# Half-height products alternated between the two row halves of TensorE, and attention scores as three float32r products

## The chip, the cores and the metric

The kernel runs on one core of a Trainium2 chip. The metric is the device time of one execution in microseconds (us); lower is better. Engines are named as in the profile: PE is TensorE's matmul stream, PEld its weight loads, DVE VectorE, ACT ScalarE, POOL GpSimd, SP the queue of SyncE that issues DMAs.

## The reference

One decoder block on 512 tokens of width 1024. A combined input projection feeds two mixers side by side, differential attention ("da", 4 heads of two 64-wide halves) and RWKV-7 time mixing ("rw", 8 heads of 64); then an output projection, a PEER retrieval over 16384 experts, an embedding gate and a last norm. What the change touches is in the mixers:

```python
# diff_attention, one block of 128 queries (h = 4 heads, c = 2 halves of 64)
s = jnp.einsum('bhcqd,bhckd->bhcqk', qb, k).astype(f32)
pr = jax.nn.softmax(jnp.where(causal, s, -jnp.inf), axis=-1)
a = pr[:, :, 0] - lam * pr[:, :, 1]
return jnp.einsum('bhqk,bhkv->bhqv', a.astype(v.dtype), v)

# rwkv7_mix, one token
sa = jnp.einsum('bhij,bhj->bhi', state, -kk_t)
state = (state * d_t[:, :, None, :] + sa[..., None] * (kk_t * a_t)[:, :, None, :]
         + v_t[..., None] * k_t[:, :, None, :])
return state, jnp.einsum('bhij,bhj->bhi', state, r_t)
```

## The kernel before

Tokens are handled in four blocks b = 0 to 3 of 128. The kernel is written in a tile framework: at build time a scheduler fixes the order of instructions on each engine, and pools hand out memory pages; a tile that is given a page used before waits for the last reader of the old tile. At run time every engine works through its own list in order. Two tags of pages carry the mixers: `p2` (128 x 512 floats, 28 pages) and `p4` (128 x 1024 floats, 14 pages).

The mixers take the first 436 us or so of the program. Up to about 142 us the rw columns are projected. Then, for each b, `rw_prepare(b)` computes decays and keys (matmuls plw, pla, pcum, prem; DVE ops e_ex, ka, zs, aa, be, kt), transposes four tiles to 64-row layout (ptr: be, e_ex, e_in, kt), multiplies them per head (psA, 64 rows each: the heads of even number use the upper row half of TensorE, s = 0, those of odd number the lower, s = 1), masks the results on DVE (aab, arb, aak, ark) and multiplies with the values (pg, copied out as akv). Matmuls acc of the da projections are woven between as filler for PE; `da_prepare(b)` applies rope and transposes queries and keys (ptq, copied into qT and kT). Psum tiles of psA, pg, py and most others share the tag "mm", which has two banks.

The triangular systems of the rw mixer are solved on DVE: `rw_solve(half)` loads both blocks' masked products (sol_u) and runs 31 steps of one multiply (sol_p) and one reduce (sol_x), one after the other, with results sent out over DRAM (td, read back as tt). `rw_solve(0)` serves b = 0, 1; the table `PACE = (0, 0, 4, 0)` offers its steps while `rw_prepare(2)` is written. `rw_solve(1)` serves b = 2, 3 and is offered with the first attention heads. Its sol_u lies in a p4 page, its sol_p in a p2 page.

From about 277 us on, per b: attention scores psS (four heads times c = 0, 1; 64-row matmul of up to 512 keys, then a 128-row matmul that adds the causal mask, then max on DVE and exp on ACT into a p4 tile pexp), pta and po for the values; and for rw: pwu, pmt, prp, then per 32-token chunk the state update pst and at the end the output py (L702 at full height, L710 on 64 rows and 32 columns). Matmuls accr of another projection are filler here.

Of the kernel before, what the change touches and what calls it, by code (L numbers as in the profile page):

```python
# [8 lines left out]
F32 = mybir.dt.float32  # L9
F32R = mybir.dt.float32r  # L10
# [8 lines left out]
T = 512  # L19
# [35 lines left out]
class Kernel:  # L55
# [347 lines left out]
    def p2(self, name, shape=(128, 512), dt=F32):  # L403
        return self.pages.tile(list(shape), dt, name=name, tag="p2", bufs=28)

    def p4(self, name, shape=(128, 1024), dt=F32):
        return self.pages.tile(list(shape), dt, name=name, tag="p4", bufs=14)
# [48 lines left out]
    def rw_prepare(self, b, psum, r, k, v, kk, lx, st):  # L456
# [85 lines left out]
        for lhs, d0, d1 in ((bet, aab, st["arb"]), (ktt, aak, ark)):  # L542
            for m2 in range(2):
                for s in range(2):
                    q = slice(64 * s, 64 * s + 64)
                    ps = psum.tile([128, 2, 2, 128], F32, name="psA", tag="mm")
                    for mm in range(2):
                        m = 2 * m2 + mm
                        nc.tensor.matmul(ps[:, mm, :, :], lhs[q, m * 128:(m + 1) * 128], art[q, m, :, :],  # L549
                                         start=True, stop=True)  # L550
                    h = slice(4 * m2 + s, 4 * m2 + s + 3, 2)
                    nc.vector.tensor_tensor(d0[:, h, :], ps[:, :, 0, :],
                                            self.mask2[:, None, 0, :].to_broadcast([128, 2, 128]), op=OP.mult)
                    nc.vector.tensor_tensor(d1[:, h, :], ps[:, :, 1, :],
                                            self.mask2[:, None, 1, :].to_broadcast([128, 2, 128]), op=OP.mult)
# [127 lines left out]
    def rw_out(self, b, st, psum, out):  # L683
# [14 lines left out]
        for par in range(2):  # L698
            py = psum.tile([128, 4, 64], F32, name="py", tag="mm")
            o = slice(64 * par, 64 * par + 64)  # L700
            for m in range(4):
                nc.tensor.matmul(py[:, m, :], st["arb"][:, 2 * m + par, :], st["wu"][:, 1, 2 * m + par, :],  # L702
                                 start=(m == 0), stop=False, skip_group_check=True)
            for c in range(4):
# [3 lines left out]
                q = slice(32 * c, 32 * c + 32)  # L708
                for m in range(4):
                    nc.tensor.matmul(py[q, m, :], st["rp"][o, m, q], s[o, m, :], start=False,  # L710
                                     stop=(m == 3), skip_group_check=True)
            nc.vector.tensor_tensor(y[:, par:8:2, :], py, yk[:, par:8:2, :], op=OP.add)
# [15 lines left out]
    def da_prepare(self, b, z, zT, psum):  # L728
# [16 lines left out]
        if isinstance(zT, list):  # L745
            for i, x in enumerate(zT):
                nc.scalar.activation(x[:, :, b * 128:b * 128 + 128], pt[:, 2 * i:2 * i + 2, :], AF.Copy)
        else:
            nc.scalar.activation(zT, pt, AF.Copy, scale=0.125)

    def da_block(self, b, qT, kT, vs, psum, out):
# [7 lines left out]
        for h in range(4):  # L759
            pq = self.p4("pexp", [128, 2, 512])  # L760
            p = [pq[:, 0], pq[:, 1]]
            for c in range(2):
                o = slice(64 * c, 64 * c + 64)
                ps = psum.tile([128, 512], F32, name="psS", tag="acc", bufs=4)
                nc.tensor.matmul(ps[:, :nk], qT[o, h, :], kT[h // 2][o, h % 2, :nk], start=True, stop=True)  # L765
                nc.tensor.matmul(ps[:, b * 128:nk], self.ident_r, self.causal, start=False, stop=True,
                                 skip_group_check=True)
                mx = st[:, c, h:h + 1]
                nc.vector.tensor_reduce(mx, ps[:, :nk], axis=AX.X, op=OP.max, negate=True)
                nc.scalar.activation(p[c][:, :nk], ps[:, :nk], AF.Exp, bias=mx, accum_out=st[:, 2 + c, h:h + 1])  # L770
# [839 lines left out]
```

## Time and profile before

| | |
|---|---|
| median of three executions | 1839.75 us (1837.05 to 1845.11) |
| profiled execution | 1837.09 us, span 1835.4 us |
| granted clock of PE, mean over the span | 0.969 |
| PE busy | 1728.9 us (94%) |
| DVE busy | 1425.6 us (78%) |
| ACT busy | 746.7 us (41%) |
| POOL busy | 604.7 us (33%) |

Busy shares are means over the whole program; the mixers are its first quarter, and only there do the two builds differ in the order of their instructions. A busy PE is not PE at its peak: records of pipelined matmuls overlap, so what a matmul costs is read from the distance between starts.

### The profile page before, as it was taken

How to read it: one execution, taken by the hardware profiler on the slowest of the kernel's cores; microseconds unless marked ns; L12 is line 12 of the kernel's file. 1: busy time of each engine (PE TensorE's matmuls, PEld its weight loads, DVE VectorE, ACT ScalarE, POOL GpSimd, SP SyncE). 2: the span in 40 equal slices, each digit the busy share in tenths (PEclk: the TensorE clock that was granted, in tenths of full speed). 3: DMA queues.
4: the chain of work that ended last, by engine and by line, in shares of the span. 5: the costliest groups of instructions: out<-in, count | busy, mean ns of one | idle time of the engine just before them, and what ended most of it. 6: DMA issues, size and time to landing. Idle time of an engine off the chain costs nothing.

```text
span 1835.4 us, 28662 instructions
## 1 busy us (share of the span) xinstructions
PE 1728.9 (94%) x10458; PEld 1468.2 (80%) x10458; DVE 1425.6 (78%) x3216; ACT 746.7 (41%) x1382; POOL 604.7 (33%) x425
## 2 busy tenths in 40 slices
PE   7889996998899888999999999999999999999998
PEld 6766764766777787998777888889899999999986
DVE  5366787675569998888888888887888888888885
ACT  5353332432345654444344333333333333333354
POOL 2650011111046663001111133234545555555530
PEclk9896996999999999999999999999999999999999
DMA  7451233433332343446666587778989898989891
GB/s 232 137 149 55 75 114 79 129 80 127 117 120 71 125 127 115 132 139 216 206 209 197 187 272 249 254 246 292 313 302 317 300 316 303 312 303 316 303 332 58
DMA packets 150417, 363.71 MB, mean 198 GB/s; under 512 B 43922, under 2 KB 58510, under 8 KB 150148
## 3 DMA queue, kind: packets, MB, share of 16 engines
q1 hardware_dynamic: 113412, 227.65, 38.7%
q0 software_dynamic: 36864, 134.23, 21.5%
q8 instruction: 82, 1.34, 0.3%
q14 instruction: 59, 0.48, 0.1%
HBM read 332.61 MB, written 21.36 MB: 193 GB/s over the span
## 4 chain that ended last, share of the span: by engine, by line
PE 67%; DVE 19%; issue 3%; ACT 3%; POOL 0%; DMA 0%; SPq 0%; DVEq 0%; ACTq 0%; POOLq 0%
PE po L1278 21%; PE phid L1142 8%; PE phid L1144 8%; PE phid L1143 8%; PE pg L1247 2%; DVE wlo L133 2%; PE psA L549 2%; DVE ids L1091 2%; ACT whi L129 1%; DVE rest L985 1%; PE psS L765 1%; DVE jj L1235 1%; PE accr L239 1%; PE accr L237 1%; PE accr L238 1%
## 5 line engine op out<-in xcount | busy, mean ns | idle before, releaser
L133 DVE TENSOR_TENSOR wlo<-wraw,whi 128x1024 fp32r<-128x1024 f32 x243 | 297.5, 1224 | 150.6 <-ACT whi L129 150.5
L129 ACT ACTIVATE whi<-wraw 128x1024 fp32r<-128x1024 f32 x276 | 291.4, 1057 | 171.3 <-PE phid L1143 59.0
L1144 PE MATMUL phid<-u2dhi,wlo 128*128 128x384 f32 x1024 | 347.3, 339 | 12.8 <-POOL wlo L133 12.8
L1142 PE MATMUL phid<-u2dhi,whi 128*128 128x384 f32 x1024 | 350.4, 342 | 1.0 <-ACT row L1151 1.0
L1143 PE MATMUL phid<-u2dlo,whi 128*128 128x384 f32 x1024 | 346.4, 338 | 0.0
L1301 POOL DMA_INDIRECT row<-in_peer_u_dram,idx x128 | 189.8, 1483 | 403.2 <-DVE row L1313 219.7
L1301 POOL DMA_INDIRECT row<-in_peer_v_dram,idx x128 | 186.1, 1454 | 277.0 <-DVE h L1317 194.7
L1278 PE MATMUL po<-whi,chi 128*128 128x512 f32 x768 | 243.9, 398 | 1.2 <-ACT row L1151 1.2
L1278 PE MATMUL po<-whi,clo 128*128 128x512 f32 x768 | 243.1, 398 | 1.7 <-DVE clo L135 0.4
L1278 PE MATMUL po<-wlo,chi 128*128 128x512 f32 x768 | 241.4, 395 | 0.0
L1144 PEld LDWEIGHTS phid<-u2dhi,wlo 128*128 128x128 f32 x1024 | 194.3, 190 | 14.8 <-POOL wlo L133 14.7
L1142 PEld LDWEIGHTS phid<-u2dhi,whi 128*128 128x128 f32 x1024 | 194.6, 190 | 5.8 <-ACT row L1151 1.3
L1143 PEld LDWEIGHTS phid<-u2dlo,whi 128*128 128x128 f32 x1024 | 194.1, 190 | 3.7
L1278 PEld LDWEIGHTS po<-whi,clo 128*128 128x128 f32 x768 | 143.0, 188 | 42.3 <-DVE clo L135 9.0
L1278 PEld LDWEIGHTS po<-wlo,chi 128*128 128x128 f32 x768 | 144.4, 188 | 34.2
L1317 DVE SCALAR_TENSOR_TENSOR h<-row,ids,h 128x1024 f32<-128x1024 f32 x128 | 164.0, 1281 | 1.6
L129 ACT ACTIVATE chi<-gelu 128x384 fp32r<-128x384 f32 x128 | 67.4, 526 | 240.1 <-DVE gelu L1255 121.8
L1278 PEld LDWEIGHTS po<-whi,chi 128*128 128x128 f32 x768 | 141.1, 188 | 25.6 <-ACT row L1151 1.5
L1313 DVE SCALAR_TENSOR_TENSOR row<-row,xn 128x1024 f32<-128x1024 f32 x128 | 153.7, 1220 | 0.0
L1151 ACT ACTIVATE gelu<-phid 128x384 f32<-128x384 f32 x86 | 42.3, 492 | 266.9 <-PE phid L1144 266.9
L133 POOL TENSOR_TENSOR wlo<-wraw,whi 128x1024 fp32r<-128x1024 f32 x33 | 78.4, 2386 | 126.4 <-ACT whi L129 114.7
L201 PE MATMUL acc<-whi,uhi 128*128 128x512 f32 (+1 forms) x224 | 89.6, 404 | 16.7 <-ACT whi L129 9.5
(439 smaller groups left out, 2884.7 us busy)
## 6 DMA issues: line engine op xcount, KB each, us to landing
wraw<-in_peer_uT_dram SPq DMA_DIRECT2D x128, 512.0 KB
wraw<-in_peer_v_dram SPq DMA_DIRECT2D x128, 512.0 KB
wraw<-in_w_in_dram SPq DMA_DIRECT2D x24, 512.0 KB
wraw<-in_peer_w_q_dram SPq DMA_DIRECT2D x16, 512.0 KB
ahead<-row SPq DMA_DIRECT2D x42, 192.0 KB
gelu<-ahead SPq DMA_DIRECT2D x42, 192.0 KB
wraw<-in_w_out_dram SPq DMA_DIRECT2D x8, 512.0 KB
zp<-z SPq DMA_DIRECT2D x12, 224.0 KB
```

What stands on the lines that cost most here:

```text
L129: self.last_hi = nc.scalar.activation(hi, src, AF.Copy, **({} if g is None else {"scale": g}))
L133: self.last_lo = eng.tensor_tensor(lo, src, hi.bitcast(F32), op=OP.subtract)
L201: nc.tensor.matmul(o, hi[:, k, s], whi, start=(k == 0), stop=False)
L549: nc.tensor.matmul(ps[:, mm, :, :], lhs[q, m * 128:(m + 1) * 128], art[q, m, :, :], start=True, stop=True)
L1142: nc.tensor.matmul(ps, whi[:, s], hi[:, k, :], start=(k == 0), stop=False)
L1143: nc.tensor.matmul(ps, whi[:, s], lo[:, k, :], start=False, stop=False)
L1144: nc.tensor.matmul(ps, wlo[:, s], hi[:, k, :], start=False, stop=(k == KC - 1))
L1151: nc.scalar.activation(g, ps, AF.Gelu)
L1278: nc.tensor.matmul(outs[b, e], lhs[:, s], rhs[:, 512 * e:512 * e + 512], start=(c == 0 and rhs is vhi and lhs is chi), stop=(c == NKEY - 1 ...
L1301: nc.gpsimd.indirect_dma_start(out=row, out_offset=None, in_=a["peer_u" if kind == "U" else "peer_v"], in_offset=bass.IndirectOffsetOnAxis ...
L1313: nc.vector.scalar_tensor_tensor(row, row, 1.0, xn0, op0=OP.mult, op1=OP.mult, accum_out=hid0[:, k:k + 1])
L1317: nc.vector.scalar_tensor_tensor(acc0, row, hid0[:, k:k + 1], acc0, op0=OP.mult, op1=OP.add)
```

## The change

Four edits. psA: both psum tiles of a pair are taken first, and the matmuls are written in turn for the upper and the lower row half. py: the same for the two parities of heads, with the 32-column chunks rotated. Scores: queries and keys are split into a float32r high part and a float32r rest (helper `split`, an ACT copy and a DVE subtraction), and each score is hi x hi + hi x lo + lo x hi, written in turn for c = 0 and 1 with a psum bank for each; the two causal additions follow both. Pages: qT takes 8 p2 pages in place of 4 and kT 4 p4 pages in place of 2; the pools are changed to 26 p2 and 15 p4, which are the same bytes. What is left for other tiles falls from 24 to 18 p2 pages and from 12 to 11 p4 pages.

```diff
@@ -401,10 +401,10 @@
         nc.scalar.activation(self.cos.rearrange("p b j -> p (b j)"), x0, AF.Sin)
 
     def p2(self, name, shape=(128, 512), dt=F32):
-        return self.pages.tile(list(shape), dt, name=name, tag="p2", bufs=28)
+        return self.pages.tile(list(shape), dt, name=name, tag="p2", bufs=26)
 
     def p4(self, name, shape=(128, 1024), dt=F32):
-        return self.pages.tile(list(shape), dt, name=name, tag="p4", bufs=14)
+        return self.pages.tile(list(shape), dt, name=name, tag="p4", bufs=15)
 
     def shift_group(self, rs, alloc, g0, n):
 
@@ -541,18 +541,21 @@
         st["arb"] = p4("arb", [128, 8, 128])
         for lhs, d0, d1 in ((bet, aab, st["arb"]), (ktt, aak, ark)):
             for m2 in range(2):
+
+                ps = [psum.tile([128, 2, 2, 128], F32, name="psA", tag="mm") for s in range(2)]
+                for mm in range(2):
+                    m = 2 * m2 + mm
+                    for s in range(2):
+                        q = slice(64 * s, 64 * s + 64)
+                        nc.tensor.matmul(ps[s][:, mm, :, :], lhs[q, m * 128:(m + 1) * 128], art[q, m, :, :],
+                                         start=True, stop=True)
                 for s in range(2):
-                    q = slice(64 * s, 64 * s + 64)
-                    ps = psum.tile([128, 2, 2, 128], F32, name="psA", tag="mm")
-                    for mm in range(2):
-                        m = 2 * m2 + mm
-                        nc.tensor.matmul(ps[:, mm, :, :], lhs[q, m * 128:(m + 1) * 128], art[q, m, :, :],
-                                         start=True, stop=True)
                     h = slice(4 * m2 + s, 4 * m2 + s + 3, 2)
-                    nc.vector.tensor_tensor(d0[:, h, :], ps[:, :, 0, :],
+                    nc.vector.tensor_tensor(d0[:, h, :], ps[s][:, :, 0, :],
                                             self.mask2[:, None, 0, :].to_broadcast([128, 2, 128]), op=OP.mult)
-                    nc.vector.tensor_tensor(d1[:, h, :], ps[:, :, 1, :],
-                                            self.mask2[:, None, 1, :].to_broadcast([128, 2, 128]), op=OP.mult)
+                    nc.vector.tensor_tensor(
+                        d1[:, h, :], ps[s][:, :, 1, :], self.mask2[:, None, 1, :].to_broadcast([128, 2, 128]),
+                        op=OP.mult)
             yield
             if lhs is bet:
 
@@ -695,21 +698,24 @@
         nc.gpsimd.tensor_tensor(bvf, bvf, self.ln_b, op=OP.add)
         y = self.p2("y", [128, 8, 64])
         yk = st["yk"].rearrange("p (h v) -> p h v", h=8)
-        for par in range(2):
-            py = psum.tile([128, 4, 64], F32, name="py", tag="mm")
-            o = slice(64 * par, 64 * par + 64)
-            for m in range(4):
-                nc.tensor.matmul(py[:, m, :], st["arb"][:, 2 * m + par, :], st["wu"][:, 1, 2 * m + par, :],
+        py = [psum.tile([128, 4, 64], F32, name="py", tag="mm") for par in range(2)]
+        for m in range(4):
+            for par in range(2):
+                nc.tensor.matmul(py[par][:, m, :], st["arb"][:, 2 * m + par, :], st["wu"][:, 1, 2 * m + par, :],
                                  start=(m == 0), stop=False, skip_group_check=True)
-            for c in range(4):
+
+        for m in range(4):
+            for i in range(8):
+                par = i % 2
+                c = (i // 2 + 2 * par) % 4
                 s = st["s"][c]
                 if s is None:
                     continue
-                q = slice(32 * c, 32 * c + 32)
-                for m in range(4):
-                    nc.tensor.matmul(py[q, m, :], st["rp"][o, m, q], s[o, m, :], start=False,
-                                     stop=(m == 3), skip_group_check=True)
-            nc.vector.tensor_tensor(y[:, par:8:2, :], py, yk[:, par:8:2, :], op=OP.add)
+                o, q = slice(64 * par, 64 * par + 64), slice(32 * c, 32 * c + 32)
+                nc.tensor.matmul(py[par][q, m, :], st["rp"][o, m, q], s[o, m, :], start=False,
+                                 stop=(m == 3), skip_group_check=True)
+        for par in range(2):
+            nc.vector.tensor_tensor(y[:, par:8:2, :], py[par], yk[:, par:8:2, :], op=OP.add)
         mean = sm.tile([128, 8], F32, name="mean")
         nc.vector.tensor_reduce(mean, y, axis=AX.X, op=OP.add)
         nc.vector.tensor_scalar(mean, mean, 1.0 / 64, None, op0=OP.mult)
@@ -742,11 +748,13 @@
         pt = psum.tile([128, 4, 128], F32, name="ptq", tag="tp")
         for h in range(4):
             nc.tensor.transpose(pt[:, h, :], z[:, h * 128:(h + 1) * 128], self.ident)
-        if isinstance(zT, list):
-            for i, x in enumerate(zT):
-                nc.scalar.activation(x[:, :, b * 128:b * 128 + 128], pt[:, 2 * i:2 * i + 2, :], AF.Copy)
+        hi, lo = zT
+        if isinstance(hi, list):
+            for i in range(2):
+                d = slice(b * 128, b * 128 + 128)
+                self.split(hi[i][:, :, d], lo[i][:, :, d], pt[:, 2 * i:2 * i + 2, :])
         else:
-            nc.scalar.activation(zT, pt, AF.Copy, scale=0.125)
+            self.split(hi, lo, pt, g=0.125)
 
     def da_block(self, b, qT, kT, vs, psum, out):
 
@@ -759,15 +767,21 @@
         for h in range(4):
             pq = self.p4("pexp", [128, 2, 512])
             p = [pq[:, 0], pq[:, 1]]
+
+            ps = [psum.tile([128, 512], F32, name="psS", tag="acc", bufs=4) for c in range(2)]
+            for i, j in ((0, 0), (0, 1), (1, 0)):
+                for c in range(2):
+                    o = slice(64 * c, 64 * c + 64)
+                    nc.tensor.matmul(ps[c][:, :nk], qT[i][o, h, :], kT[j][h // 2][o, h % 2, :nk],
+                                     start=i + j == 0, stop=i == 1)
             for c in range(2):
-                o = slice(64 * c, 64 * c + 64)
-                ps = psum.tile([128, 512], F32, name="psS", tag="acc", bufs=4)
-                nc.tensor.matmul(ps[:, :nk], qT[o, h, :], kT[h // 2][o, h % 2, :nk], start=True, stop=True)
-                nc.tensor.matmul(ps[:, b * 128:nk], self.ident_r, self.causal, start=False, stop=True,
+                nc.tensor.matmul(ps[c][:, b * 128:nk], self.ident_r, self.causal, start=False, stop=True,
                                  skip_group_check=True)
+            for c in range(2):
                 mx = st[:, c, h:h + 1]
-                nc.vector.tensor_reduce(mx, ps[:, :nk], axis=AX.X, op=OP.max, negate=True)
-                nc.scalar.activation(p[c][:, :nk], ps[:, :nk], AF.Exp, bias=mx, accum_out=st[:, 2 + c, h:h + 1])
+                nc.vector.tensor_reduce(mx, ps[c][:, :nk], axis=AX.X, op=OP.max, negate=True)
+                nc.scalar.activation(p[c][:, :nk], ps[c][:, :nk], AF.Exp, bias=mx,
+                                     accum_out=st[:, 2 + c, h:h + 1])
 
             f = sm.tile([128, 1], F32, name="smf")
             nc.vector.reciprocal(f, st[:, 3, h:h + 1])
@@ -872,7 +886,8 @@
                     self.mark = self.last_hi
             self.rope_tables(cpool, cpool)
             self.lambdas(cpool)
-            zd, qT, kT, vs = {}, {}, [p4(f"kT{i}", [128, 2, T]) for i in range(2)], {}
+            zd, qT, kT, vs = {}, {}, [[p4(f"kT{x}{i}", [128, 2, T], F32R) for i in range(2)]
+                                  for x in ("hi", "lo")], {}
 
             def eat_z(b, ps):
                 zd[b] = p2("z")
@@ -889,7 +904,7 @@
                     yield from self.proj_steps(psum, hi, lo, w, 512 * i, 512, eat, g=g)
                     for b in range(NB) if i < 2 else ():
                         if i == 0:
-                            qT[b] = p2("qT", [128, 4, 128])
+                            qT[b] = [p2(f"qT{x}", [128, 4, 128], F32R) for x in ("hi", "lo")]
                         self.da_prepare(b, zd[b], kT if i else qT[b], psum)
                         if b % DAP == DAP - 1:
                             yield
```

**DVE, first half of rw_prepare(2).** What stands between the last op on e_ex and the op on be, which PE transposes first. sol_p and sol_x are the steps of rw_solve(0), wlo a split for the da projection. Before:

```order
L593 TENSOR_TENSOR sol_p<-sol_x,sol_u 128x2
L500 SCALAR_TENSOR_TENSOR ka<-aa,b_rw_k_a 128x512
L595 TENSOR_REDUCE sol_x<-sol_p 128x1
L135 SCALAR_TENSOR_TENSOR wlo<-wraw,g_mix,whi 128x512
L593 TENSOR_TENSOR sol_p<-sol_x,sol_u 128x3
L502 SCALAR_TENSOR_TENSOR zs<-ka,zs 128x512
```

Of the change, the same place begins like this:

```order
L135 SCALAR_TENSOR_TENSOR wlo<-wraw,g_mix,whi 128x512 x2
L506 TENSOR_TENSOR e_in<-zs,e_in 128x512
L504 SCALAR_TENSOR_TENSOR e_ex<-kk,e_ex 128x512
L596 TENSOR_TENSOR sol_p<-sol_x,sol_u 128x2
L598 TENSOR_REDUCE sol_x<-sol_p 128x1
```

and ka comes after the last of the solve's 62 rows, with four rows of wlo among them:

```order
L596 TENSOR_TENSOR sol_p<-sol_x,sol_u 128x512
L598 TENSOR_REDUCE sol_x<-sol_p 128x16
L500 SCALAR_TENSOR_TENSOR ka<-aa,b_rw_k_a 128x512
L502 SCALAR_TENSOR_TENSOR zs<-ka,zs 128x512
L507 TENSOR_TENSOR aa<-aa,kk 128x512
L510 TENSOR_TENSOR be<-aa,e_inv 128x512
```

In the old build ka and the solve's first step are neighbours and the two chains alternate; in the new one ka is given the p2 page of rw_solve(0)'s sol_p, and so stands behind the whole solve. On PE, between plw of b = 2 and the transposition of be, there stood 40 matmuls acc, and now 54; between that transposition and the second pg of b = 3 there stood 97, and now 72.

**POOL, ahead of rw_solve(1).** The memset of sol_u (the ones on its diagonal) is the last thing that the solve's first step waits for on POOL; wlo here is a split of another projection's weights. Before, and then of the change:

```order
L606 MEMSET tt 128x1024
L584 MEMSET sol_x 128x512
L588 MEMSET sol_x 64x16 x2
L133 TENSOR_TENSOR wlo<-wraw,whi 128x1024
L589 MEMSET sol_u 128x32
```

```order
L133 TENSOR_TENSOR wlo<-wraw,whi 128x1024
L592 MEMSET sol_u 128x32
L587 MEMSET sol_x 128x512
L591 MEMSET sol_x 64x16 x2
L133 TENSOR_TENSOR wlo<-wraw,whi 128x1024
```

One wlo moved from ahead of the memset to behind it, another stays ahead.

**PE, scores of b = 2, first two heads.** 974 is a tile of high parts of the keys (of the keys themselves in the old build), 976 one of their rests. Before, and then of the change:

```order
L765 MATMUL psS<-kT_974,qT 128x384
L766 MATMUL psS<-causal_r,ident_r 128x128
L765 MATMUL psS<-kT_974,qT 128x384
L766 MATMUL psS<-causal_r,ident_r 128x128
L688 MATMUL plg<-g_up,lg 128x512
```

```order
L775 MATMUL psS<-kThi_974,qThi 128x384 x2
L775 MATMUL psS<-kTlo_976,qThi 128x384 x2
L775 MATMUL psS<-kThi_974,qTlo 128x384 x2
L778 MATMUL psS<-causal_r,ident_r 128x128 x2
L691 MATMUL plg<-g_up,lg 128x512
L704 MATMUL py<-wu,arb 128x64 x3
L775 MATMUL psS<-kThi_974,qThi 128x384
L775 MATMUL psS<-kTlo_976,qThi 128x384
L775 MATMUL psS<-kThi_974,qTlo 128x384
L775 MATMUL psS<-kThi_974,qThi 128x384
L775 MATMUL psS<-kTlo_976,qThi 128x384
L775 MATMUL psS<-kThi_974,qTlo 128x384
```

The causal matmul of c = 0 no longer stands between the 64-row matmuls of the two halves. The first head's are in turn (x2), the second's stand half after half. In eight of the twelve heads of b = 1 to 3 the 64-row matmuls of both halves are neighbours, in turn or half after half; in two of b = 1 and two of b = 3 a full-height matmul stands between the halves.

## Rows read from the trace of the kernel before

**Rows 1.** DVE around 204 us, timeline: start, duration, line, tile.

```profile
203.75 0.16 DVE L593 TENSOR_TENSOR sol_p<-sol_x,sol_u 128x2 f32<-128x2 f32 x1
203.82 0.69 DVE L500 SCALAR_TENSOR_TENSOR ka<-aa,b_rw_k_a 128x512 f32<-128x512 f32 x1
...
204.49 0.74 DVE L135 SCALAR_TENSOR_TENSOR wlo<-wraw,g_mix,whi 128x512 fp32r<-128x512 f32 x1
...
207.30 0.68 DVE L510 TENSOR_TENSOR be<-aa,e_inv 128x512 f32<-128x512 f32 x1
```

**Rows 2.** PE, timeline, blocks 2 and 3; brackets: idle before, and what ended it.

```profile
210.03 0.39 PE L202 MATMUL acc<-wlo,uhi 128*128 128x512 f32 x1
210.26 0.60 PE L531 MATMUL ptr<-ident,be 128*128 128x128 f32 x4
...
234.51 0.63 PE L744 MATMUL ptq<-ident,z 128*128 128x128 f32 x4 [2.03 <-DVE z L741]
235.97 0.63 PE L744 MATMUL ptq<-ident,z 128*128 128x128 f32 x4 [0.83 <-ACT kT L747]
...
237.90 2.07 PE L475 MATMUL plw<-w_up,lw 65*128 65x512 f32 x2 [0.98 <-DVE lw L471]
```

**Rows 3.** Chain of waits, 200 to 316 us: start, duration, what.

```profile
273.60 0.61 ACT akv L571
...
278.93 2.35 POOL wlo L133
...
301.26 12.32 issue
```

**Rows 4.** By stretch: us, busy us of PE, PEld, DVE, ACT, POOL (instructions), clock, DMA, GB/s.

```profile
236.80:243.60 6.80, 5.82 (x9) 2.44 (x8) 5.93 (x17) 4.75 (x7) 0.00 (x0) 0.50 0.08 8
...
299.70:308.50 8.80, 8.78 (x20) 5.91 (x21) 6.58 (x14) 0.98 (x5) 0.00 (x0) 0.50 0.00 1
...
326.00:408.00 82.00, 79.64 (x855) 57.25 (x855) 60.09 (x194) 31.44 (x81) 12.12 (x10) 0.98 0.46 117
408.00:436.00 28.00, 23.43 (x328) 19.44 (x328) 19.85 (x69) 11.76 (x22) 1.72 (x1) 1.00 0.07 11
```

**Rows 5.** DVE by line, 281 to 316 us: count, busy us, mean ns, idle before.

```profile
L593 DVE TENSOR_TENSOR sol_p<-sol_x,sol_u 128x2 f32<-128x2 f32 (+30 forms) x31 | 15.4, 498 | 1.9 <-POOL sol_u L589 1.0
L595 DVE TENSOR_REDUCE sol_x<-sol_p 128x1 f32<-128x2 f32 (+30 forms) x31 | 10.6, 342 | 0.9
```

**Rows 6.** PE, timeline, psA of block 3; each line is eight records of four matmuls.

```profile
261.51 1.14 PE L549 MATMUL psA<-art,beT 64*128 64x256 f32 x8
...
263.58 1.76 PE L549 MATMUL psA<-art,beT 64*128 64x256 f32 x8 [0.50 <-DVE arb L554]
```

**Rows 7.** DVE, timeline, masks of one such group of psA.

```profile
264.72 0.42 DVE L552 TENSOR_TENSOR aab<-psA,mask 128x256 f32<-128x256 f32 x1 [0.62 <-PE psA L549]
265.06 0.42 DVE L554 TENSOR_TENSOR arb<-psA,mask 128x256 f32<-128x256 f32 x1
```

**Rows 8.** PE, timeline, scores of b = 1 and b = 3, states and outputs of rw.

```profile
326.65 0.70 PE L765 MATMUL psS<-kT,qT 64*128 64x256 f32 x2
327.27 0.33 PE L766 MATMUL psS<-causal_r,ident_r 128*128 128x128 f32 x1
327.53 0.70 PE L765 MATMUL psS<-kT,qT 64*128 64x256 f32 x2
...
394.92 0.63 PE L710 MATMUL py<-state,rtT 64*32 64x64 f32 x8
395.48 0.68 PE L667 MATMUL pst<-uv,bk 64*64 64x64 f32 x16
395.99 0.63 PE L675 MATMUL pst<-state,mt 64*64 64x64 f32 x16
```

**Rows 9.** Chain of waits, 314 to 440 us: scores of b = 2 and of b = 3.

```profile
351.76 0.84 PE psS L765 x2
...
374.85 1.05 PE psS L765 x2
```

## The prediction

> **What bounds the kernel now.** The two builds list the same instructions in the same order behind the mixers, so I look for the change only between 142 and 436 us and take the rest as shifted as a whole. I read the chain of waits first, then the timelines of DVE and PE where it changes engine, then busy time and clock by stretch. There are two regimes. Up to 314 us, PE and DVE hold each other: DVE alternates ops of rw_prepare with steps of rw_solve(0), one for one [rows 1]; PE waits little, three stops of 2.03, 0.83 and 0.98 us [rows 2], and 236.8 to 243.6 at half clock [rows 4]; then rw_solve(1) keeps DVE, and ACT's exp waits 12.32 us for the page of its sol_u [rows 3]. From 326 to 408 us PE is the bound: busy 79.64 of 82.00 us, DVE 60.09 [rows 4]. There a matmul saved is a matmul gained; before it only what ends a wait counts.
>
> **The change part by part.** The sum goes along the time axis.
>
> *Pages: the stall.* In the new order ka stands behind all 62 steps of rw_solve(0) and four wlo. The first step starts at 203.75 [rows 1]; two wlo that have moved ahead of it cost little since e_ex waits for ACT anyway, I add 0.5. The solve alone is read from rw_solve(1): busy 15.4 + 10.6 = 26.0 us and idle of 0.9 + 0.9 between its ops, leaving out the 1.0 for sol_u [rows 5]: 27.8 us. A wlo takes 0.74, and its successor starts 0.66 after it: four make 2.6. Then ka, zs, aa and be, four ops of 0.68 that overlap by some 0.08: 2.5. So be is there at 203.75 + 0.5 + 27.8 + 2.6 + 2.5 = 237.2; before, it ended at 207.98 [rows 1] and PE came to it at 210.26 [rows 2]. PE's cover is 14 more matmuls acc than before, 0.23 each (210.03 to 210.26 [rows 2]), 3.3 us: PE runs dry at 213.5 and stands for 23.7 us. What is queued behind the transposition on PE, all of blocks 2 and 3, starts 26.9 us late. Nothing can hide this: DVE takes its list in order.
>
> *What is given back by akv of block 3.* Before, 210.26 to 273.60 is 63.3 us [rows 2, 3]. Taken off: the three stops, 3.8, and one of 0.50 [rows 6], since DVE is free of the solve; half of the 6.8 us at half clock, 3.4; and 25 matmuls acc fewer in that stretch, 5.8. That leaves 49.8. Put on: clock after the stall. PE stood before 299.72 and then ran at 0.50 for 8.8 us [rows 4], which is worth up to 4.4; I take 3, since the first matmuls wait for copies. The rests of kT, eight DVE ops like a mask of 0.42 [rows 7] ahead of the next copies of ptq, put on 1.5 (bounds 0 and 3.4). psA takes off 1 at most (below). Sum 53.3: akv starts at 237.2 + 53.3 = 290.5, 16.9 late.
>
> *rw_solve(1).* From akv at 273.60 it took 7.7 us to the end of a POOL wlo at 278.93 + 2.35 = 281.28 [rows 3], and the memset behind it freed the solve. That wlo now stands behind the memset; what the memset still waits for is sol_u's DMA. The gain is 0 if that lands as late as the wlo ended, 2.35 if it had landed when the wlo began, and up to 5 if soon after akv; I take 2.7. The solve starts and ends 14.2 late, and with it the page that the 12.32 us wait was for. So the PE-bound stretch starts 14.2 us late (bounds 10 and 18).
>
> *psA.* 64 matmuls, nothing removed. The group at 261.51 had both banks free and was written half after half; its eight records took 1.14 us, against 1.76 for a group that had to wait for masks in between [rows 6]. So PE overlaps the halves already without being told. In the new order only the first of four groups per block has both halves in turn; the others still wait for DVE, whose masks of a group start 0.34 apart, 1.36 for four [rows 7]. I take 0.25 to 0.5 per later block, the 1 us above.
> The Trainium skill ("TensorEngine Tiling (Array Packing)", Theoretical Speedup) states up to twice the speed where the contraction is 64 or less; taken alone that would halve psA, eight groups of 1.76 in blocks 2 and 3, some 7 us as an estimate. The same page (PSUM Bottleneck) states that evacuation does not get faster with it; by the rows above that decides, and the sum keeps 1.
>
> *Scores.* From the first 64-row record of a half to the causal matmul it takes 0.62 at 256 keys [rows 8], 0.84 at 384 and 1.05 at 512 [rows 9]; times eight halves each: 20.1 us for b = 1 to 3. A float32r matmul of 512 columns (acc) is worth 0.23 [rows 2], so 0.12, 0.17 and 0.23 by length. Three of them overlapping with the other half's three cost 0.35, 0.52 and 0.69 per head, without overlap twice that. Two heads of b = 1, four of b = 2 and two of b = 3 overlap: 2 x 0.35 + 2 x 0.70 + 4 x 0.52 + 2 x 0.69 + 2 x 1.38 = 8.3. Saved 11.8 (bounds: 0.3, if a 64-row float32r record costs as much as one of the two old records of a half; 13.9, if all overlap). One change of array height fewer per head, 0.1 each: 1.2. The scores of b = 0 lie under rw_solve(1) and count nothing.
>
> *py.* 240 records of L710; eight in 0.56 us before pst, while pst, in turn over tiles, needs 0.51 for sixteen [rows 8]. At the pst rate the long runs would save about 5; single py matmuls now stand between scores and cost more changes of tile. I take 3 (bounds 0 and 6).
>
> *After 326.* PE has 16 us less to do. Not all of it is time: uv's DMAs, exp and the state updates, now covered by shorter scores, show as waits, and 408 to 436 was not PE-bound before (23.43 of 28.00 [rows 4]). I take 4 for new waits: 12 gained (bounds 5 and 17).
>
> *Sum.* +14.2 - 12 = +2.2 us on the profiled execution's 1837.1 (span 1835.4, and 1.7 around it): 1839.3. That execution lies 2.7 below the median, so for a median: 1842.
>
> **The rivals.** *The starvation of pages goes on (slower).* Behind 326 us 18 p2 pages serve what had 24: POOL's bv, the DMAs into bhr and ykr and the states wait for pages' readers; one head of b = 0 already stands behind rw_solve(1)'s page where it did not. If that costs 8 of the 12, it is +10.2: 1850; with 5 gained against a shift of 18 it is +13, 1853. Over 0.5% (9.2 us) it comes when shift minus gain passes 9.2. For it: DVE and PE held each other before 314, so little slack is there; against it: 326 to 408 shows PE full, and page waits there were covered.
>
> *The halves do not overlap (the change doesn't do what it says).* Then scores cost 12.5 in place of 8.3, py saves nothing, and the gain is some 7: +7, 1847. Against it: rows 6 show both halves at work at once.
> The Trainium skill ("FP8 and Floating Point Precision", TensorE Precision Notes) counts four passes for true float32; three products in place of four passes save a quarter where nothing overlaps. By it 20.1 would become 15.1, a gain of 5.0 as an estimate, and the time would lie 2.6 above this rival's. The trace bears the count out: 0.92 for four times 0.23, where a half took 1.05 with its changes of height.
>
> *The stall is given back and the scores give all (faster).* If kT's rests and the clock cost nothing, the shift is 14.2 - 4.5 = 9.7; with 17 gained it is -7.3: 1832. It passes 0.5% when another 2 us go, of the 4.6 that PE stood in 408 to 436 or of sol_u's wait. For it: the stall comes once, the savings in every head.
>
> **How the numbers follow.** The forecast's case, 0.45; starvation going on, 0.25; no overlap, 0.12; all given back, 0.18. About 0.5% is what a measurement of this kernel can tell from no change. The forecast's case and that of no overlap lie inside it for the most part; starvation is mostly beyond it, and so are parts of the other two when their shift is at its upper bound; of the faster case a good half is beyond. That makes 0.14 faster, 0.56 the same, 0.30 slower. The range takes in the lower end of the last rival and the upper bound of the first: 1828 to 1858.
>
> **What would show it.** Right: PE idle for 20 to 26 us in one piece from about 213 us, ended by be on DVE; clock at half (1.2 of 2.4 GHz) behind it; akv of block 3 at 290, rw_solve(1) from about 295; the first wait-free stretch from about 328; scores at 384 keys in turn at about 0.5 per head before the causal matmuls; PE no longer full from 340 to 422. Wrong: no such gap (then the shift falls away, and 12 gained make 1828), or a gap as long with a second one behind 326 (then 1850 and more). If the gap is there and akv comes before 285, the part that is given back was mis-sized.

## The result

The change makes the kernel slower: 1860.88 us against 1839.67, medians of four runs each, ratio 1.0105 (95% interval 1.007 to 1.0141). The forecast was 1842 with a range up to 1858. The profiled execution took 1862.98 us (span 1861.3, granted clock 0.954 against 0.969), 25.9 more than that of before; it is the slowest of the four (the others had 0.958 to 0.962).

The pause stands where it was forecast. DVE of the changed kernel (start, duration; to be set against [rows 1]): the solve's last step, then ka to be.

```profile
235.67 0.69 DVE L598 TENSOR_REDUCE sol_x<-sol_p 128x16 f32<-128x512 f32 x1
236.40 0.69 DVE L500 SCALAR_TENSOR_TENSOR ka<-aa,b_rw_k_a 128x512 f32<-128x512 f32 x1
...
238.45 0.69 DVE L510 TENSOR_TENSOR be<-aa,e_inv 128x512 f32<-128x512 f32 x1
```

PE of the changed kernel, timeline, brackets as in [rows 2]; then the copy of akv on ACT (to be set against [rows 3]) and the first step of rw_solve(1); last, of before, that step and PE's wait for exp:

```profile
214.20 0.39 PE L203 MATMUL acc<-whi,ulo 128*128 128x512 f32 x1
239.19 1.11 PE L531 MATMUL ptr<-ident,be 128*128 128x128 f32 x4 [24.60 <-DVE be L510]
...
314.44 0.48 PE L792 MATMUL pta<-ident,pexp 128*128 128x128 f32 x1 [3.64 <-DVE pexp L789]
...
327.82 0.47 PE L775 MATMUL psS<-kThi,qThi 64*128 64x128 f32 x1 [6.55 <-ACT pexp L783]
...
396.10 0.55 PE L792 MATMUL pta<-ident,pexp 128*128 128x128 f32 x3 [1.50 <-DVE pexp L789]
...
431.28 0.63 PE L792 MATMUL pta<-ident,pexp 128*128 128x128 f32 x4 [1.46 <-DVE pexp L789]
```

```profile
289.76 0.60 ACT L574 ACTIVATE akv<-pg 128x512 f32<-128x512 f32 x1 [1.19 <-PE pg L572]
...
296.92 0.16 DVE L596 TENSOR_TENSOR sol_p<-sol_x,sol_u 128x2 f32<-128x2 f32 x1 [11.41 <-POOL sol_x L591]
```

```profile
281.41 0.16 DVE L593 TENSOR_TENSOR sol_p<-sol_x,sol_u 128x2 f32<-128x2 f32 x1 [0.97 <-POOL sol_u L589]
...
314.09 0.79 PE L765 MATMUL psS<-kT,qT 64*128 64x128 f32 x2 [4.47 <-ACT pexp L770]
```

PE stands for 24.60 us; akv of block 3 is 16.2 late (289.76, before 273.60); the wait for exp ends at 327.82, 13.7 later than the 314.09 of before. Behind it the forecast fails. The changed kernel by stretch (columns as in [rows 4]):

```profile
219.40:243.30 23.90, 4.11 (x18) 3.40 (x20) 22.90 (x37) 2.09 (x4) 0.00 (x0) 0.50 0.13 31
308.20:342.30 34.10, 23.89 (x140) 17.16 (x141) 22.64 (x50) 3.48 (x14) 0.00 (x0) 0.50 0.15 38
342.30:424.30 82.00, 74.64 (x825) 57.40 (x824) 57.47 (x180) 31.44 (x83) 12.13 (x10) 0.85 0.46 120
```

34.1 us in one piece at half clock (1.2 of 2.4 GHz), with PE's waits of 3.64 and 6.55 us in it, and a mean of 0.85 in the 82 us behind it, where [rows 4] had 0.98. The scores themselves are short. One head of b = 2 in the changed kernel (to be set against [rows 9]):

```profile
374.69 0.44 PE L775 MATMUL psS<-kThi,qThi 64*128 64x384 f32 x2
374.97 0.34 PE L775 MATMUL psS<-kTlo,qThi 64*128 64x384 f32 x2
375.14 0.33 PE L775 MATMUL psS<-kThi,qTlo 64*128 64x384 f32 x2
375.41 0.44 PE L778 MATMUL psS<-causal_r,ident_r 128*128 128x128 f32 x2
```

0.72 us to the causal matmuls for both halves (375.41 - 374.69), against 0.84 for one half. The next head, whose halves stand one after the other, takes 1.07 (377.30 to 378.37).

### The profile page after: what moved, and what is told of

The parts are those of the page before. It is cut to its first block, busy times and chain, and to the rows that moved or that the text cites. A ratio compares the mean times of both kernels' runs of the same rounds, so it can differ in the third digit from the quotient of the medians.

```text
span 1861.3 us, 28747 instructions
## 1 busy us (share of the span) xinstructions
PE 1731.3 (93%) x10490; PEld 1476.1 (79%) x10490; DVE 1444.9 (78%) x3228; ACT 747.3 (40%) x1382; POOL 605.7 (33%) x425
## 4 chain that ended last, share of the span: by engine, by line
PE 51%; DVE 15%; issue 2%; ACT 2%; POOL 0%; DVEq 0%; ACTq 0%; POOLq 0%
PE po L1293 21%; PE phid L1157 8%; PE phid L1159 8%; PE phid L1158 8%; PE pg L1262 2%; DVE wlo L133 2%; DVE ids L1106 1%; ACT whi L129 1%; DVE rest L1000 1%; DVE jj L1250 1%; DVE si L1002 1%; DVE si L998 1%; DVE gelu L1270 1%; PE accr L1447 1%; PE accr L1448 1%
## 5 line engine op out<-in xcount | busy, mean ns | idle before, releaser
L1316 POOL DMA_INDIRECT row<-in_peer_v_dram,idx x128 | 185.8, 1451 | 277.0 <-DVE h L1332 195.0
L1159 PEld LDWEIGHTS phid<-u2dhi,wlo 128*128 128x128 f32 x1024 | 195.5, 191 | 14.7 <-POOL wlo L133 14.7
L1293 PEld LDWEIGHTS po<-whi,clo 128*128 128x128 f32 x768 | 143.3, 188 | 41.7 <-DVE clo L135 8.7
```

Of the source, the lines that this page charges most:

```text
L1159: nc.tensor.matmul(ps, wlo[:, s], hi[:, k, :], start=False, stop=(k == KC - 1))
L1293: nc.tensor.matmul(outs[b, e], lhs[:, s], rhs[:, 512 * e:512 * e + 512], start=(c == 0 and rhs is vhi and lhs is chi), stop=(c == NKEY - 1 ...
L1316: nc.gpsimd.indirect_dma_start(out=row, out_offset=None, in_=a["peer_u" if kind == "U" else "peer_v"], in_offset=bass.IndirectOffsetOnAxis ...
```

## The experiments

Two measures serve all of them. From each kernel's one trace: **to scores**, from the first ptr of block 1 (179.6 us before) to the first psS (277.0), and **attention**, from there to the first tps of the output projection (427.3), with the granted clock and PE's idle time of that stretch. From its timed runs: the median, and the means of **time x clock** (time by mean granted clock) and of **clock lost** (the rest; time at half clock counts half, also where PE idles). The kernel before was timed with each group; its medians were 1837.1, 1837.5, 1837.2 and 1837.8, and its means here are over all 101 runs. Runs of one kernel differ mostly in clock: over these 101 the standard deviation is 7.2 us of clock lost and 2.8 of time x clock, and the mean granted clock lies between 0.959 and 0.975. So a clock read from one trace is one draw; the last two columns weigh more.

| kernel | median us (runs) | ratio, 95% | to scores | attention | its clock | PE idle in it | time x clock | clock lost |
|---|---|---|---|---|---|---|---|---|
| before | 1837.5 (101) | 1 | 97.4 | 150.3 | 0.89 | 18.9 | 1780.4 | 57.3 |
| the change | 1860.9 (4) | 1.007 to 1.0141 | 113.8 | 154.6 | 0.80 | 23.7 | 1782.1 | 77.7 |
| pages alone | 1870.0 (5) | 1.016 to 1.0216 | 115.6 | 164.4 | 0.79 | 18.0 | 1791.5 | 78.9 |
| pages, no pause | 1843.8 (12) | 1.0018 to 1.0059 | 98.1 | 162.1 | 0.81 | 19.3 | 1779.7 | 64.7 |
| small products alone | 1840.0 (12) | 0.9982 to 1.0031 | 96.5 | 156.5 | 0.81 | 19.2 | 1775.0 | 63.6 |
| scores alone (with pages) | 1868.7 (5) | 1.0157 to 1.0215 | 114.2 | 158.0 | 0.83 | 23.0 | 1788.0 | 80.4 |
| change, no pause | 1846.1 (12) | 1.0029 to 1.0069 | 100.8 | 160.3 | 0.78 | 26.4 | 1775.3 | 71.7 |
| products twice | 1870.0 (6) | 1.016 to 1.0215 | 113.9 | 164.2 | 0.82 | 23.2 | 1792.0 | 78.9 |
| float32 scores in turn | 1837.9 (12) | 0.9976 to 1.0019 | 96.7 | 153.6 | 0.78 | 20.3 | 1771.2 | 65.5 |
| filler in a wait | 1850.6 (9) | 1.0046 to 1.01 | 100.6 | 160.1 | 0.81 | 21.6 | 1778.1 | 72.2 |
| before, no maximum | 1833.2 (12) | 0.9955 to 1.0005 | 100.4 | 149.8 | 0.87 | 18.5 | 1778.2 | 56.0 |
| float32 in turn, no maximum | 1827.2 (12) | 0.9906 to 0.9959 | 96.7 | 143.3 | 0.85 | 20.5 | 1769.1 | 59.0 |
| change, no pause, no maximum | 1832.5 (12) | 0.9956 to 1.0009 | 100.7 | 144.2 | 0.83 | 22.5 | 1772.7 | 61.1 |
| before, maximum twice | 1849.0 (12) | 1.0042 to 1.0091 | 97.4 | 163.9 | 0.81 | 20.0 | 1783.2 | 66.1 |
| change, no maximum | 1844.0 (12) | 1.0005 to 1.0052 | 113.5 | 146.9 | 0.81 | 19.2 | 1781.5 | 63.5 |

### The parts: pages, small products, scores, and the change without the pause

Pages alone, edited in before:

```diff
-        return self.pages.tile(list(shape), dt, name=name, tag="p2", bufs=28)
+        return self.pages.tile(list(shape), dt, name=name, tag="p2", bufs=22)
-        return self.pages.tile(list(shape), dt, name=name, tag="p4", bufs=14)
+        return self.pages.tile(list(shape), dt, name=name, tag="p4", bufs=13)
```

> The kernel before with its two kinds of pages cut to 22 and 13, which leaves the other tiles as many as the change does; scores, mask products and py as before. Theory 1 (the late pages make the pause at 214 to 239 us and cost 14 us; the further 8 to 12 are lost behind it because TensorE, with less to do between its waits, falls to half its clock): the pause of about 24 us is there, the first scores of 256 columns come about 14 us late, TensorE's clock from there to 440 us stays as before (about 9 us of clock lost from 314 to 500 us), and the time is 1848 to 1856. Theory 2 (the late pages are the whole of it): 1857 to 1865, with 25 us or more of clock lost from 314 to 500 us. Theory 3 (the shorter products make TensorE fall to half clock, pages or not): 1848 to 1856, as theory 1.

Small products: before with the psA and py parts of the change's diff.

> The kernel before with the mask products and py of the change alone; scores and pages as before. Theory 1: the pairs run at once and up to 4 us are saved, 1835 to 1840. Theory 2: the same. Theory 3: what is saved is lost again in TensorE's clock, 1840 to 1848.

Scores alone: the change without those two parts.

> The changed kernel with the mask products and py of before: split keys and queries with their pages, scores as three products. Theory 1: the pause and the lost clock stay, 1858 to 1865, within 4 us of the changed kernel. Theory 2: the same. Theory 3: about half of the loss is gone with the small products, 1850 to 1857.

The change with the solve's two work tiles in one p4 page:

```diff
-        x, pr = (self.p2(y, [128, 16, 32]) for y in ("sol_x", "sol_p"))
+        xp = self.p4("sol_xp", [128, 2, 16, 32])
+        x, pr = xp[:, 0], xp[:, 1]
```

> The changed kernel with the two half-size work tiles of the triangular solve put into one page of the larger kind, so that ka of the third block no longer waits for the solve's page and the solve's steps stand between the other rows of VectorE as before. Theory 1: the pause at 214 us goes and with it 14 us; the shorter products alone still cost some clock: 1834 to 1848. Theory 2: all of the loss goes and the shorter scores show as a gain: 1824 to 1834. Theory 3: only the pause goes; 314 to 500 us still loses over 25 us of clock: 1846 to 1852.

Measured: pages alone cost 32.5 us, more than the whole change; theory 2 put the loss down to them and still fell short, by 5 us. With the products in, 9.1 of it come back (1870.0 to 1860.9; 9.4 of time x clock). Scores alone are as slow as pages alone (1868.7), against theory 3 and 4 us above the range of theories 1 and 2. Without the pages the small products give nothing that can be measured, between theories 1 and 3: time x clock falls by 5.4, and 6.3 more clock is lost. Without the pause the change takes 14.8 us less and is still 9 us slower than before, which the times of theories 1 and 3 allow and theory 2 does not (of the over 25 us of clock that theory 3 has lost from 314 to 500 us, the trace shows 24).

### Is the lost clock due to TensorE having less to do, or waiting?

Each product twice, in the change:

```diff
-            for i, j in ((0, 0), (0, 1), (1, 0)):
+            for i, j in ((0, 0), (0, 1), (1, 0)) * 2:
```

> The changed kernel with each of the three score products issued twice (the second set starts the sums again). At full clock that is some 7 us more of matmuls on TensorE (per pair of halves about 0.25, 0.35, 0.5 and 0.67 us for 128, 256, 384 and 512 columns, four heads each). Theory 1 (behind the pause the time is lost in TensorE's clock, which falls where TensorE waits): the clock lost, which is the time multiplied by one minus the mean granted clock, falls by about what the extra matmuls add, and the time stays within 4 us of the changed kernel, 1857 to 1865. Rival (TensorE's work sets the time behind the pause): the whole 7 us show, 1866 to 1870, with the clock lost as in the changed kernel, about 78 us.

Pages without the pause: the edits of the first and the fourth kernel together, in before.

> The kernel before with 22 and 13 pages, and the two work tiles of the triangular solve in one page of the larger kind, so that the pause at 214 us should not come; scores and small products as before. Theory 1 (the pause, and the clock that TensorE has behind it, are what the late pages cost): 1837 to 1845. Rival (fewer pages delay the stretch behind 314 us by themselves, pause or not): 1850 to 1857.

Filler: the change with the solve in one page, and at the head of py in rw_out

```diff
+        if b == 0:
+            for _ in range(40):
+                nc.tensor.matmul(py[0].rearrange("p m v -> p (m v)"), self.ident_r, self.fill, start=True, stop=True)
```

where fill is 256 columns of the keys' high part.

> The changed kernel with the solve's tiles in one page, and 40 useless matmuls of 256 columns put ahead of py of the first block, where TensorE waited 2.9 and 9.0 us at 296 to 310 us (8.5 us of matmuls at half clock, 4.3 at full): they lie in a wait and end before it. Theory 1 (TensorE's clock falls because it waits): the granted clock is back at full before 310 us instead of at 324, the clock lost falls by 5 us or more, and the time is 2 to 8 us under that of the kernel with the solve in one page, 1838 to 1844. Rival (the clock falls for another reason, or the low clock behind the wait costs nothing): the clock there stays, and the time is within 2 us of that kernel, 1844 to 1848.

Measured: the doubled products show in full, 9 us, and the clock lost is 78.9 against 77.7 (two standard errors 6.8, as the change has four runs): theory 1 fell here, the rival holds. The filler lay in the wait, as PE's timeline shows,

```profile
297.17 6.55 PE L705 MATMUL py<-kThi,ident_r 128*128 128x256 f32 x40 [2.79 <-DVE rtT L655]
303.56 1.00 PE L708 MATMUL py<-wu,arb 128*128 128x64 f32 x8
308.33 0.70 PE L237 MATMUL accr<-whi,phi 128*128 128x512 f32 x1 [3.77 <-ACT pexp L787]
```

and brought nothing over the program: 72.2 us of clock lost against 71.7, median 4.5 higher, above both expectations (the means differ by 3.2 us, two standard errors 3.7). On the spot the clock did move in its trace (columns as in [rows 4]):

```profile
301.60:308.40 6.80, 3.03 (x27) 2.90 (x25) 6.50 (x9) 0.58 (x3) 0.00 (x0) 1.00 0.00 0
308.50:311.70 3.20, 3.20 (x9) 2.18 (x10) 0.73 (x3) 0.69 (x4) 0.00 (x0) 0.50 0.00 0
```

The change without the pause has 0.50 from 301.6 to 308.4. Here the clock is full behind the first part of the filler and falls again behind the 3.77 us that PE still waits for exp. So the wait was only partly filled, and that waits cost clock is not excluded by this run; shown is that neither the work added nor this filler gave clock back over the program. Pages without the pause cost 6.3 us, as theory 1 had it, so the pause is worth 26.3 there (1870.0 to 1843.8), 17.5 of it ahead of the first scores (115.6 and 98.1). The 6.3 are clock: time x clock is that of before. The attention stage of that kernel, and in it one piece (columns as in [rows 4]):

```profile
271.90:434.00 162.10, 142.79 (x1425) 103.99 (x1425) 109.34 (x322) 48.48 (x128) 17.15 (x13) 0.81 0.32 83
...
379.70:400.20 20.50, 20.50 (x134) 13.65 (x133) 7.38 (x16) 3.02 (x9) 0.95 (x1) 0.50 0.27 68
```

PE stays at half clock for 20.5 us while the profile shows it busy all along; half of that, 10.25, is nearly the 11.8 by which the stage is longer than before.

### Float32 scores in turn

Before with the small products, both halves' float32 products ahead of both causal ones, a bank each, 28 and 14 pages:

```diff
+            ps = [psum.tile([128, 512], F32, name="psS", tag="acc", bufs=4) for c in range(2)]
+            for c in range(2):
+                o = slice(64 * c, 64 * c + 64)
+                nc.tensor.matmul(ps[c][:, :nk], qT[o, h, :], kT[h // 2][o, h % 2, :nk], start=True, stop=True)
```

> The kernel before with the mask products and py of the change, and with the two float32 score products of a head issued one behind the other, a bank for each, ahead of both causal products; no split, the 28 and 14 pages of before. Theory 1 (halves in different rows run at once in float32 too; no page is late): up to 8 us of TensorE's time saved in the scores and 6 in the small products, part of it lost again in the clock: 1826 to 1836. Rival (float32 halves do not overlap, only the split ones do): as with the small products alone, 1836 to 1842.

PE in that kernel, a head of b = 2:

```profile
346.82 0.92 PE L771 MATMUL psS<-kT,qT 64*128 64x384 f32 x4
347.67 0.44 PE L773 MATMUL psS<-causal_r,ident_r 128*128 128x128 f32 x2
```

0.85 us for both float32 halves (347.67 - 346.82), where one took 0.84 alone and the three split products take 0.72 for both: nearly all of the gain in such a head comes from the order, and needs no page. This bears out the Trainium skill ("TensorEngine Tiling (Array Packing)", Theoretical Speedup: up to twice the speed at a contraction of 64 or less). Not every head of b = 2 gains as much: the fourth takes 0.84 (362.83 to 363.67), the second 1.25 (349.56 to 350.81). The time is that of before all the same: time x clock falls by 9.2 us, and 8.2 more clock is lost. The stage's clock is 0.78, and a piece like the one above is there too:

```profile
346.80:375.40 28.60, 27.15 (x336) 20.15 (x336) 22.53 (x72) 10.55 (x29) 7.97 (x6) 0.94 0.45 118
375.40:395.90 20.50, 20.50 (x127) 12.78 (x126) 7.77 (x14) 3.45 (x9) 3.21 (x3) 0.50 0.34 82
```

### Is it VectorE's softmax?

Float32 in turn, before, the change without the pause, and the change, each without the row maximum, here in before's form:

```diff
-                mx = st[:, c, h:h + 1]
-                nc.vector.tensor_reduce(mx, ps[:, :nk], axis=AX.X, op=OP.max, negate=True)
-                nc.scalar.activation(p[c][:, :nk], ps[:, :nk], AF.Exp, bias=mx, accum_out=st[:, 2 + c, h:h + 1])
+                nc.scalar.activation(p[c][:, :nk], ps[:, :nk], AF.Exp, accum_out=st[:, 2 + c, h:h + 1])
```

> The kernel before with the small products of the change and its float32 scores in turn, and without the row maximum (32 reductions of VectorE in the softmax): the exponentials follow the scores directly, with no shift. Theory V (TensorE, once shortened, runs into VectorE's softmax, waits, and drops to half clock; with VectorE relieved the saving shows): 6 us or more under the kernel before without its row maximum. Theory C (what TensorE saves comes back as lost clock whatever VectorE does): within 4 us of the kernel before without its row maximum, with 6 us or more of clock lost beyond that kernel's.

> The kernel before without the row maximum of the scores: the exponentials follow the scores directly, with no shift; nothing else is changed. It is the base for the two kernels beside it. Both theories: VectorE has some 14 us less to do, the waits of TensorE for the exponentials of the first block at 300 and 314 us get shorter, 1822 to 1837.

> The changed kernel with the solve's tiles in one page (no pause), and without the row maximum: the exponentials follow the scores directly, with no shift. Theory V: 4 us or more under the kernel before without its row maximum, as the shorter products now show. Theory C: 2 to 10 us over it, as it was with the row maximum.

> The changed kernel without the row maximum: the exponentials follow the scores directly, with no shift; the pause at 214 us stays. Theory V: against the kernel before without its row maximum only the pause is left, some 14 us: 1844 to 1851. Theory C: all of the loss is left, some 23 us: 1853 to 1860.

The other way, in before: the row maximum taken twice (`for _ in range(2):` ahead of it).

> The kernel before with each row maximum taken twice: VectorE has 32 reductions and 15.6 us more to do in the softmax, TensorE the same work and pages as before. Theory V (TensorE loses its clock where VectorE's softmax makes it wait): half clock of 10 us or more appears from 351 to 427 us, the clock lost rises by 5 us or more over the kernel before, 1843 to 1860. Theory C (the clock falls only where TensorE's own work is shorter): the stretch keeps its full clock, and the time rises only by what is on the path, 1837 to 1843.

And before once more, unchanged:

> The kernel before once more, unchanged, for a second trace. If the full clock that its trace showed from 349 to 438 us belongs to the kernel, this trace shows at most one short piece at half clock there; if it was chance, 10 us or more at half clock, as the traces with shorter products had, may stand there.

Measured: the maximum is worth 4.3 us in the kernel before, 10.7 with float32 scores in turn, 13.6 in the change without the pause, 16.9 in the change. In the last two it is nearly all clock lost (10.6 of 13.2 and 14.2 of 14.8, by the means). Float32 in turn then lies 6.0 under before without the maximum (difference of means 6.1, two standard errors 3.8), where V had 6 or more, and the change 10.8 over it (1844.0), at the lower edge of V's range. The change without the pause is level with it (0.7 under), between V's 4 and C's 2. With the maximum twice the kernel before loses 11.5 us, as V had it, 8.8 of them clock, though its TensorE has the same work, partly in another order: in its trace this piece is new,

```profile
383.60:400.70 17.10, 17.10 (x93) 10.59 (x91) 7.86 (x14) 1.86 (x4) 3.22 (x3) 0.50 0.36 93
```

which theory C excluded. But V's own reason, that TensorE waits more, does not show: PE's idle in the stage is 20.0 us against 18.9, and in the 7.2 us ahead of this piece PE is no less busy than where before has nearly the same products (pwu, pmt, prp). First the maximum twice, then before:

```profile
376.40:383.60 7.20, 6.67 (x99) 5.38 (x100) 6.65 (x25) 4.36 (x12) 0.00 (x0) 1.00 0.12 19
```

```profile
377.00:384.20 7.20, 6.46 (x104) 5.40 (x104) 6.55 (x24) 4.25 (x12) 0.00 (x0) 1.00 0.12 18
```

Behind the first the clock falls, behind the second it stays full. Of the kernel before, the first trace's attention stage, and behind it the second trace's, with its second half:

```profile
277.00:427.30 150.30, 131.36 (x1425) 97.51 (x1424) 106.08 (x323) 47.80 (x128) 17.23 (x14) 0.89 0.37 88
```

```profile
271.10:421.30 150.20, 131.69 (x1426) 97.65 (x1425) 106.02 (x323) 47.74 (x128) 17.27 (x14) 0.88 0.38 87
...
345.60:421.30 75.70, 72.28 (x931) 53.47 (x929) 52.84 (x165) 24.97 (x63) 11.19 (x9) 1.00 0.35 81
```

By what was expected of the second trace, the higher clock belongs to the kernel: 0.89 and 0.88, full from b = 2 on, and its two measures are 97.4 and 150.1. The second trace is of a short execution (1831.02 us, 0.974); no run of before at 0.959 to 0.961, of which there are seven, was traced, and such a piece may stand in them.

The fastest of these kernels is float32 in turn without the maximum: 1827.2, ratio 0.9933 to before (0.9906 to 0.9959). It leaves out the shift that keeps the exponentials small whatever the scores are.

## Why the prediction was wrong

**The pause: right.** be at 238.45 + 0.69 = 239.1 (237.2 forecast), PE idle for 24.60 (23.7), akv 16.2 late (16.9), rw_solve(1) 15.5 late (296.92 against 281.41 before; 14.2 forecast). Removing it gave 14.8 us, close to the shift that was forecast; that this agrees so well is in part luck, since in the kernel with fewer pages alone it gave 26.3.

**Scores and small products: right in mechanism; the small products gave more, the scores less.** The halves overlap, so that rival fell. 32 records of py, before and in the change:

```profile
370.72 1.39 PE L710 MATMUL py<-state,rtT 64*32 64x64 f32 x32
```

```profile
426.08 0.65 PE L715 MATMUL py<-state,rtT 64*32 64x64 f32 x32
```

psA and py took 5.4 us off time x clock where 1 and 3 stood in the sum. The scores took 3.5 (scores alone against pages alone) to 3.8 (float32 in turn against small products alone), where 11.8 and 1.2 stood. A head of 384 keys was put at 0.52 in turn and took 0.72; with the pages, PE's idle in the attention stage rose from 18.0 to 23.0 us.

**The step that failed is "After 326": 4 for new waits, 12 gained.** Up to there the forecast holds: PE's wait for exp ends 13.7 late, 14.2 forecast. Solve and products were to shorten the attention stage by 14.7 (2.7 and 12); it grew by 4.3. (With the 16.4 before it that makes 20.7 of the 25.9 between the two profiled executions; 1.9 lie ahead of these stretches and 3.3 behind them.) The products, waits included, gave 9.1 against pages alone, not far from 12. The price that the sum lacked is TensorE's clock in that stage, 0.80 for 0.89: of its 154.6 us 30.9 are lost, of the 150.3 before 16.5, which is 14.4 more. Fewer pages alone bring it to 0.81 without any pause, with PE's idle as before (19.3 and 18.9). The stage of the changed kernel:

```profile
295.30:449.90 154.60, 130.94 (x1458) 101.15 (x1457) 109.65 (x330) 48.21 (x128) 17.62 (x17) 0.80 0.36 87
```

I read [rows 4] as "a matmul saved is a matmul gained"; that would hold at the granted clock of that stretch, 0.98, which I carried over. DVE, busy for 60.09 of 82.00 us there, was taken for slack; one row maximum more in its softmax in before, or one less in the change, moved the clock of TensorE.

**The rival nearest to the result** is starvation of pages, 1850 to 1853: its place is right, its mechanism, waits for pages' readers, at most a part. In the changed kernel PE's waits from 345 to 440 us, among them (us in total, times, longest)

```profile
PE pta L792 <- DVE pexp L789: 3.0, 2, 1.5
PE pmt L646 <- DMA bhr<-d_bh: 2.0, 1, 2.0
PE po L805 <- ACT ah L796: 1.3, 2, 0.7
```

sum to 10.4 us, against 3.8 from 328 to 424 before: 6.6 more, where 4 stood. Which of them stem from a late page the list does not tell.

**Open.** What starts and ends the pieces at half clock. Fewer pages, shorter products and a longer softmax each bring them (stage clock 0.78 to 0.83 against 0.89 and 0.88); without the maximum it is 0.83 to 0.87, but 0.81 in the change with its pause, which all the same gains 16.9 us. Over many runs the clock lost says the same (63.6 to 80.4 us against 57.3). That the softmax makes TensorE stop and so fall to half clock is not shown, and the two rows of 7.2 us speak against it; shown is that one row maximum more in before, or one less in the change, moves the clock and the time. Each edit also gave the scheduler a new order for the lists of the engines, and no run separates the order from the load, or from the pages.

## What to carry to other kernels

Two products that use different halves of the array's rows overlap in float32 too, if they stand next to each other with a bank each: reorder before you split, since the split's second copies cost pages and here the pages cost more (32.5 us) than the products gave (9.1). Cost a page taken from a pool by the order of the next build: which step now stands behind which page's reader. And a stretch that shows TensorE full at full clock is not a promise of what a saving there is worth: work out the saving, then measure what the clock does with it, comparing time x clock and clock lost over many runs; here more or less work on the engine beside it (VectorE's softmax) changed both.

## What the hardware showed

TensorE ran 20.50 us at half clock without a gap between its records (20.50 busy of 20.50, in two kernels; where records end is modelled by the profile). The Trainium skill ("TensorE: Matmul & The Clock Gate", Part 1: The HAM clock gate) says that the throttled state is the default and that activity releases it; in these two stretches the clock stayed at half although the profile shows TensorE as wholly busy. Forty extra matmuls in a wait were followed by 6.8 us at full clock, where the kernel without them has half, and left the clock lost over the program where it was, 72.2 against 71.7 us. Executions of one and the same kernel differ by up to 30 us of clock lost (45.7 to 76.0 over 101 runs of before).
